# State-space input tables made on GpSimd, and the chunk inputs moved behind the last input projections

## Chip, cores and metric

One core of a Trainium2 chip runs the whole two-layer model in one launch. The metric is the device time of one execution in microseconds. Rows of the profile call the engines PE (TensorE matmul; PEld its weight loads), DVE (VectorE), ACT (ScalarE), POOL (GpSimd) and SP (the queue that issues most DMAs). Each engine runs its own instructions in order, and waits on semaphores for the others.

## The reference

Only layer 0 is touched. There, 1024 latent tokens and 256 context tokens are normalised and modulated (scale and shift from a conditioning vector times a weight matrix `ada_w`), then projected by `w_in`. Columns 0 to 767 of the projection feed a bidirectional state-space recurrence (S5) with 48 groups of 16 channels and 64 complex states, columns 768 to 1023 an FNet branch, columns 1024 to 2047 a SiLU gate.

```python
lam_bar = jnp.exp(lam * step)
b_bar = ((lam_bar - 1.0) / lam)[..., None] * lax.complex(b_re, b_im)
bu = lax.complex(einsum('btgh,gph->btgp', u, b_bar.real), einsum('btgh,gph->btgp', u, b_bar.imag))
_, s = lax.associative_scan(_linear_recurrence, (a, bu), axis=1)
return einsum('btgp,ghp->btgh', s.real, c_re) - einsum('btgp,ghp->btgh', s.imag, c_im)
...
y = concat([glu(gelu(y_s5)), fnet(u_f)]) * silu(z)
xl = xl + gate * (y @ w_out)
```

## The kernel before

The recurrence is done by chunks of 8 tokens. For each group there are **input tables** (powers of `lam_bar` times `b_bar`: 8 tokens of a chunk to the chunk's contribution to the state, tile `bl`) and **output tables** (powers times C, tile `cl`, with strips of the kernel within a chunk, `z`). Twelve input tasks (`bl_task`, 4 groups each) make five element-wise operations of 128x512 on VectorE, then TensorE transposes the result (`pt`), ScalarE copies it (`bltw`) and a DMA stores it to DRAM (`bltd`). Twelve output tasks (`cl_task`) make five operations of 128x576 on VectorE, store `cl` (`cld`), and TensorE multiplies (`pz`); ScalarE and two small VectorE operations (`dg`, `z`) finish the strips. A chunk input (`bl_mm`, twelve) loads a table (`blt`) and the projected tokens (`ub`) again, multiplies them (`vps`), and ScalarE writes the chunk's contribution to `va` (groups 0 to 23) or `vb` (24 to 47).

The order is written out by hand: instructions stand on each engine's queue in the order of the Python calls. In layer 0:

1. First phase: x is loaded, the sums of squares are taken, the coefficients are computed in small VectorE operations between larger ones (`self.inter` with counts), the modulation weights are loaded and multiplied (`ada_mm`), and projections m = 0 and 1 are made as the channel tiles become ready (`first`).
2. Projections m = 2 to 5 of the S5 columns: 8 parts (k) of six 128x512 matmuls each, 48 in all, since weights and data are split into high and low halves (`whi`, `wlo`; `hh`, `hl`) for accuracy; the weight of the next projection is split on ScalarE and VectorE (`w_split`). Each is followed by the context's product (`uc`). Between the parts `fill()` runs a task's TensorE part and starts the next task, first the twelve input tasks, then the twelve output tasks, with two in flight:

```python
def fill():
    flush()
    if len(pend) == 2 or not todo:
        if pend:
            pend.pop(0)()
    if todo:
        f, b, hf = todo.pop(0)
        ...
```

3. The first FNet projection `fx(0)` with the first six chunk inputs between its parts, then the other six alone.
4. Tree and scan on VectorE: `tree` merges the context's chunks, `step` advances one chunk of one half of the groups; 121 pairs of steps stand behind the second FNet projection `fx(1)` and the eight gate projections (m = 8 to 15) on TensorE. Splits for these run on GpSimd.
5. Output stage (`yps`), which needs the last scan step; then the FNet, the GLU and layer 1, which the change leaves alone.

Weights come through a ring of four buffers (`raw`); six of the first loads have places of their own (`self.place`, tiles `hh2` to `hh7` before these are needed).

Of the kernel before, what the change touches and what calls it, by code (L numbers as in the profile page):

```python
# [30 lines left out]
# ------------------------------------------------------------------ constants that depend on shapes  # L31
# [151 lines left out]
class Builder:  # L183
# [64 lines left out]
    # ---------------------------------------------------------------- streamed weights  # L248
# [51 lines left out]
    def w_issue(self, upto=-1):  # L300
        """Loads: those that the ring has room for or that have a place of their own, and all up to the given one."""
# [23 lines left out]
    def w_split(self, name, eng=None, hi=None, lo=None, parts=1, c0=0, c1=None):  # L325
        """The stationary tile's exact high and low parts (columns c0 .. c1, of those that were left)."""
# [44 lines left out]
    # ---------------------------------------------------------------- accurate exp on DVE  # L371
# [20 lines left out]
    def cmul(self, orr, oi, ar, ai, br, bi, t1, t2):  # L392
        self.mul(t1, ar, br)
        self.mul(t2, ai, bi)
        self.mul(orr, ar, bi)
        self.mul(oi, ai, br)
        self.add(oi, oi, orr)
        self.sub(orr, t1, t2)

    # ---------------------------------------------------------------- S5 tables  # L400
    def s5_prelim(self, tp, s5s, raw):
# [21 lines left out]
        self.ts(sh, sh, -2.0, 1.0, ALU.mult, ALU.add)  # L423
        pw = tp.tile([P, 4, 9, NG], F32, name="pw")
        nc.vector.memset(pw[:, 0, 0], 1.0)
        nc.vector.memset(pw[:, 3, 0], 0.0)
# [4 lines left out]
        w2 = tp.tile([P, 4, NG], F32, name="w2")  # L431
        for n in (1, 2, 4):
# [7 lines left out]
            self.cmul(o[0], o[1], a[0], a[1], b(pw[:, 0, n]), b(pw[:, 3, n]), u1, u2)  # L440
        self.sub(pw[:, 1], pw[:, 3], pw[:, 0])
        self.add(pw[:, 2], pw[:, 3], pw[:, 0])
        # (lam_bar - 1) / lam
        den, xr, cr, ci = step, r, th, er
        self.mul(den, lre, lre)
        self.mul(t1, lim, lim)
        self.add(den, den, t1)
        nc.vector.reciprocal(den, den)
        self.ts(xr, lr, -1.0, None, ALU.add)
        self.mul(cr, xr, lre)  # L450
        self.mul(t1, li, lim)
        self.add(cr, cr, t1)
        self.mul(cr, cr, den)
        self.mul(ci, li, lre)
        self.mul(t1, xr, lim)
        self.sub(ci, ci, t1)
        self.mul(ci, ci, den)
        self.bb = self.kp.tile([P, 2, NG + 1, 16], F32, name="bb")
        self.bbs = self.gp.tile([P, NG, 16], F32, name="bbs")

        def inputs():
            """B times (lam_bar - 1) / lam, and the sum of its parts: the operations, one by one."""
            nc.vector.memset(self.bb[:, :, NG], 0.0)
            bbr, bbi = self.bb[:, 0, 0:NG], self.bb[:, 1, 0:NG]
            x = [tp.tile([P, T], F32, tag="sq", name="x1", bufs=2)[:, 0:NG * 16].rearrange("p (g h) -> p g h", g=NG)
                 for _ in range(2)]
            br, bi = (x.unsqueeze(2).to_broadcast([P, NG, 16]) for x in (cr, ci))
            for out, a, b, op in ((bbr, raw[:, 0], br, ALU.mult), (x[0], raw[:, 1], bi, ALU.mult),
# [8 lines left out]
        self.pwc = self.kp.tile([P, 3, 9, NG], F32, name="pwc")  # L477
        self.acf = self.pwp.tile([P, 2, 2, NG], F32, name="acf")

        def tables(i):  # L480
            for ri in range(3):
                if i == 0:
                    self.act(self.pwb[0:64, ri], pw[0:64, ri, 0:8][:, ::-1])
                    self.act(self.pwb[64:128, ri], pw[64:128, ri, 0:8])
# [6 lines left out]
        return tables, inputs  # L491

    def bl_task(self, b, hf):
        """Chunk input matrices of 4 groups, transposed, to DRAM: (vector part, tensor part)."""
# [4 lines left out]
        def dve():  # L499
            p = self.gt.tile([P, 4, 16, 8], F32, tag="blp", name="blp", bufs=1)  # L500
            B = [x[:, g4].unsqueeze(3).to_broadcast([P, 4, 16, 8]) for x in (self.bbs, self.bb[:, 0], self.bb[:, 1])]
            W = [self.pwb[:, i, :, g4].rearrange("p s g -> p g s").unsqueeze(2).to_broadcast([P, 4, 16, 8])
                 for i in range(3)]
# [228 lines left out]
    def layer0(self, es):  # L732
# [187 lines left out]
        for x in rest:  # L920
            if not isinstance(x, int):
                x()
# [700 lines left out]
```

## Time and profile before

| | us |
|---|---|
| median of 3 runs (lowest, highest) | 947.33 (946.02, 950.22) |
| span of the profiled execution | 943.4 |
| TensorE busy | 888.9 (94%) |
| VectorE busy | 589.4 (62%) |
| ScalarE busy | 315.9 (33%) |
| GpSimd busy | 93.8 (10%) |

The profile is of one execution; the median of the runs lies 3.9 us above its span, which holds the instructions from the first to the last. Busy shares are averages over stages with different limits, so they are read stage by stage. A row of the busy times by stage gives the stretch, its length, then us and number of instructions for PE, PEld, DVE, ACT and POOL, the granted TensorE clock, the DMA share and GB/s. A row of the timeline gives start, duration of the group, engine, line of the kernel, operation, output<-inputs, shapes, count and, in brackets, the idle time before it with what ended it.

### The profile page before, as it was taken

The page shows a single profiled execution, that of the slowest core. Times are in us where ns is not written, and L with a number is a line of the kernel's source. Part 1 is how long each engine was busy: PE and PEld are TensorE (multiplying, and loading weights), DVE is VectorE, ACT ScalarE, POOL GpSimd, SP SyncE. Part 2 cuts the span into 40 slices and gives each one's busy share as a digit, 9 for nine tenths or more (in the row PEclk, how much of TensorE's full clock was granted, in tenths as well). Part 3 has the DMA queues.
Part 4 walks back from the last instruction along what each step waited for, and adds up shares of the span by engine and source line. Part 5 has one row for each costly group of instructions (what it writes and reads, how often), then busy time and mean ns, then how long its engine had stood idle before and what let it go on. Part 6 is the DMA issues. An engine that isn't in the chain of part 4 may idle for free.

```text
span 943.4 us, 13977 instructions
## 1 busy us (share of the span) xinstructions
PE 888.9 (94%) x5432; PEld 725.6 (77%) x5432; DVE 589.4 (62%) x1563; ACT 315.9 (33%) x535; POOL 93.8 (10%) x91
## 2 busy tenths in 40 slices
PE   8998788898999958899999999999999999999996
PEld 3666566677777748887888999877888888888995
DVE  7788998767999996656367476254321343335355
ACT  5546331346212109744342244212111222233110
POOL 0002221131221303200043000100000000000000
PEclk9999999999999988999999999999999999999998
DMA  9734557994455466931162010201111111111022
GB/s 348 283 134 144 186 171 206 261 358 157 157 201 187 185 210 192 312 138 40 67 263 94 1 42 4 79 23 57 56 38 52 45 45 45 50 64 44 1 90 89
DMA packets 57601, 120.75 MB, mean 128 GB/s; under 512 B 5248, under 2 KB 30000, under 8 KB 57408
## 3 DMA queue, kind: packets, MB, share of 16 engines
q1 hardware_dynamic: 50672, 96.06, 30.2%
q0 software_dynamic: 6864, 23.81, 8.0%
q8 instruction: 42, 0.69, 0.3%
q14 instruction: 23, 0.19, 0.1%
HBM read 95.83 MB, written 24.02 MB: 127 GB/s over the span
## 4 chain that ended last, share of the span: by engine, by line
PE 62%; DVE 24%; DMA 6%; ACT 5%; issue 1%; SPq 1%; DVEq 0%; POOL 0%; ACTq 0%; POOLq 0%
PE acc L360 53%; DVE va L206 11%; DVE bl L206 4%; DVE vb L206 2%; DMA mt<-zd 2%; PE acc L867 2%; ACT vb L231 1%; DMA zd<-z 1%; DVE blp L206 1%; PE yps L1189 1%; ACT sy L231 1%; DVE xt L206 1%; PE pps L1509 1%; DMA ub<-ud 1%; PE rsb L682 1%
## 5 line engine op out<-in xcount | busy, mean ns | idle before, releaser
L360 PE MATMUL acc<-hh,whi 128*128 128x512 f32 (+1 forms) x672 | 211.8, 388 | 1.4 <-ACT whi L231 1.4
L360 PE MATMUL acc<-hl,whi 128*128 128x512 f32 (+1 forms) x672 | 207.1, 382 | 0.0
L360 PE MATMUL acc<-hh,wlo 128*128 128x512 f32 (+1 forms) x672 | 206.7, 381 | 0.1
L360 PEld LDWEIGHTS acc<-hh,whi 128*128 128x128 f32 x672 | 122.7, 188 | 30.4 <-issue 5.8
L360 PEld LDWEIGHTS acc<-hh,wlo 128*128 128x128 f32 x672 | 125.1, 188 | 25.9 <-DVE wlo L206 0.5
L360 PEld LDWEIGHTS acc<-hl,whi 128*128 128x128 f32 x672 | 125.2, 188 | 25.5
L206 DVE TENSOR_TENSOR wlo<-raw,whi 128x1024 fp32r<-128x1024 f32 (+2 forms) x47 | 52.3, 1118 | 50.9 <-ACT whi L231 50.9
L231 ACT ACTIVATE whi<-raw 128x1024 fp32r<-128x1024 f32 (+2 forms) x55 | 53.9, 986 | 50.2 <-issue 29.0
L206 DVE TENSOR_TENSOR va<-va 128x48 f32<-128x48 f32 (+1 forms) x258 | 55.9, 218 | 0.4
L227 DVE SCALAR_TENSOR_TENSOR xl<-acc,adac,xl 128x256 f32<-128x256 f32 (+1 forms) x48 | 27.3, 570 | 41.6 <-PE acc L360 41.3
L360 PE MATMUL acc<-yh,hh 128*128 128x256 f32 (+1 forms) x144 | 46.3, 321 | 0.0
L360 PE MATMUL acc<-hh,wl 128*128 128x256 f32 (+1 forms) x144 | 46.1, 320 | 0.0
L360 PE MATMUL acc<-hh,wh 128*128 128x256 f32 (+1 forms) x144 | 46.0, 320 | 0.0
L360 PE MATMUL acc<-yl,hh 128*128 128x256 f32 (+1 forms) x144 | 45.8, 318 | 0.0
L360 PE MATMUL acc<-yh,hl 128*128 128x256 f32 (+1 forms) x144 | 45.7, 317 | 0.0
L360 PE MATMUL acc<-hl,wh 128*128 128x256 f32 (+1 forms) x144 | 45.6, 317 | 0.0
L1189 PE MATMUL yps<-cl,sy 128*128 128x128 f32 x192 | 32.3, 295 | 12.7 <-ACT sy L231 12.7
L206 DVE TENSOR_TENSOR va<-va,acf 128x96 f32<-128x96 f32 x127 | 38.7, 305 | 0.2
L1189 PEld LDWEIGHTS yps<-cl,sy 128*128 128x128 f32 x192 | 28.0, 210 | 13.2 <-ACT sy L231 13.0
L231 ACT ACTIVATE hh<-xl 128x256 f32<-128x256 f32 (+1 forms) x24 | 11.7, 489 | 70.2 <-DVE xl L227 70.2
L206 DVE TENSOR_TENSOR va<-vb,acf 128x96 f32<-128x96 f32 x127 | 34.2, 269 | 0.2
L1026 PE MATMUL vps<-ub,blt 128*64 128x160 f32 x192 | 28.3, 301 | 3.9 <-DMA ub<-ud 2.5
(264 smaller groups left out, 1630.7 us busy)
## 6 DMA issues: line engine op xcount, KB each, us to landing
raw<-in_ada SPq DMA_DIRECT2D x44, 512.0 KB, 6.2
raw<-in_win SPq DMA_DIRECT2D x38, 512.0 KB, 3.6
raw<-in_wout SPq DMA_DIRECT2D x16, 512.0 KB, 3.5
bltd<-bltw POOLq DMA_DIRECT2D x12, 512.0 KB, 3.2
blt<-bltd SPq DMA_DIRECT2D x12, 512.0 KB, 8.6
cl<-cld POOLq DMA_DIRECT2D x12, 512.0 KB, 6.4
cld<-cl SPq DMA_DIRECT2D x18, 256.0 KB, 4.3
ub<-ud SPq DMA_DIRECT2D x12, 384.0 KB, 7.4
```

The lines of the kernel that those rows point to most:

```text
L206: (eng or self.nc.vector).tensor_tensor(out, a, b, op=op)
L227: self.nc.vector.scalar_tensor_tensor(out, a, s, b, op0=op0, op1=op1)
L231: self.nc.scalar.activation(out, a, func, **kw)
L360: self.nc.tensor.matmul(p, a[:, w], b[:, c0:c1], start=(j == 0 and i == 0), stop=(last and i == 2))
L682: self.nc.tensor.matmul(p2[:, P * i:P * i + P], self.ones, dg[:, i], start=True, stop=True)
L867: nc.tensor.matmul(acc[m][h], a[:, w], b[:, 512 * h:512 * h + 512], start=(k == 0 and i == 0), stop=(k == 7 and i == 2))
L1026: nc.tensor.matmul(ps[0:64, o], blt[:, ri, g, 0:64], ub[:, g, 0:160], start=True, stop=True)
L1189: nc.tensor.matmul(ps[:, o], sy[:, ri, g], cl[:, ri, g], start=False, stop=(ri == 1))
L1509: nc.tensor.matmul(ps, pwt[:, i], pd[:, 4 * h:4 * h + 4].rearrange("p s j -> p (s j)"), start=True, stop=True)
```

## The change

- The coefficient operations of `s5_prelim` behind the sine and the exponential (25, and nine small ones in `inputs`) and the seven of 768 elements that scale B run on GpSimd (`g`), only a reciprocal stays on VectorE. The counted list after `sumsq7` becomes a plain list, in which `inverse`, `inputs` and `tables(0)` have places.
- The twelve input tasks' element-wise part runs on GpSimd. It starts with two tasks; each transposition (`bl_pe`) starts the next task but one. The table of powers is held with the 8 tokens innermost (`pwb`).
- Input and output tasks are two lists, with places by projection and part (`hooks`); an output task starts when the one before it is multiplied.
- Chunk inputs move: the first six behind the parts of `fx(1)`, the others behind parts 0 to 5 of gate projection 8, two loads ahead instead of three. The second half's tree stands behind part 6, and the paired steps begin with projection 9.
- All first-phase modulation weights have places of their own (14 instead of 6); squares go to the `wlo` buffers.
- Stores of tables, projections and FNet inputs are issued by ScalarE instead of GpSimd; output tables' and strips' stores stay on SP throughout.

```diff
-        self.mul(lr, er, sh)
-        self.mul(li, er, sn)
+        self.mul(lr, er, sh, g)
+        self.mul(li, er, sn, g)
...
             for out, a, b, op in ((bbr, raw[:, 0], br, ALU.mult), (x[0], raw[:, 1], bi, ALU.mult),
...
-                self.tt(out, a, b, op)
-                yield
+                self.tt(out, a, b, op, g)
...
-        self.pwb = self.gp.tile([P, 3, 8, NG], F32, name="pwb")
+        self.pwb = self.gp.tile([P, 3, NG, 8], F32, name="pwb")
...
-            self.mul(p, B[0], W[0])
-            self.mul(bl[:, 0], B[2], W[2])
-            self.mul(bl[:, 1], B[1], W[1])
-            self.sub(bl[:, 0], p, bl[:, 0])
-            self.add(bl[:, 1], p, bl[:, 1])
+            self.mul(p, B[0], W[0], eng)
+            self.mul(bl[:, 0], B[2], W[2], eng)
+            self.mul(bl[:, 1], B[1], W[1], eng)
+            self.sub(bl[:, 0], p, bl[:, 0], eng)
+            self.add(bl[:, 1], p, bl[:, 1], eng)
...
-            nc.gpsimd.dma_start(self.bltd[b][:, :, 4 * hf:4 * hf + 4], blt)
+            nc.scalar.dma_start(self.bltd[b][:, :, 4 * hf:4 * hf + 4], blt)
...
-        for i in range(6):
-            self.place[4 + i] = self.hl_tile(f"hh{2 + i}", F32)
+        places = ["hl1", "hh1"] + [f"h{i}{k}" for k in range(2, KD) for i in "hl"]
+        places[4:6] = places[5:3:-1]
+        for i, n in enumerate(places):
+            self.place[4 + i] = self.hl_tile(n, F32)
...
+        def bl_ew():
+            if bls:
+                t = self.bl_task(*bls.pop(0))
+                t[0](nc.gpsimd)
+                blp.append(t[1])
+
+        def bl_pe():
+            blp.pop(0)()
+            bl_ew()
...
+        def cl_next():
             flush()
-            if len(pend) == 2 or not todo:
-                if pend:
-                    pend.pop(0)()
-            if todo:
-                f, b, hf = todo.pop(0)
...
+            if clp:
+                clp.pop(0)()
+            if cls:
+                t = self.cl_task(*cls.pop(0))
                 t[0]()
-                pend.append(t[1])
+                clp.append(t[1])
...
+        hooks = {2: at(k6=[cl_next], k7=[bl_pe]),
+                 3: at(k1=[cl_next], k2=[bl_pe], k4=[cl_next], k6=[cl_next], k7=[bl_pe]),
+                 4: at(k1=[cl_next], k3=[bl_pe], k4=[cl_next], k6=[cl_next]),
+                 5: at(k0=[bl_pe], k1=[cl_next], k3=[cl_next], k5=[bl_pe], k6=[cl_next])}
...
-            nc.gpsimd.dma_start(um[:, :, 32:160], ut.rearrange("p (s j) -> p s j", s=8))
+            nc.scalar.dma_start(um[:, :, 32:160], ut.rearrange("p (s j) -> p s j", s=8))
...
-            if i + 3 < 12:
-                bl_load(i + 3)
+            if i + 2 < 12:
+                bl_load(i + 2)
...
+        fx(0, at(k0=[cl_next], k1=[bl_pe], k2=[cl_next], k3=[bl_pe], k5=[lambda: bl_load(0)], k6=[bl_pe],
+                 k7=[lambda: bl_load(1)]))
+        while clp:
+            cl_next()
...
+        fx(1, at(k0=[bl_next], k1=[bl_pe], k2=[bl_next], k3=[bl_next], k4=[bl_pe], k5=[bl_next], k6=[bl_next],
+                 k7=[bl_next]))
...
-                      hook=lambda k: self.bg(2 if k % 4 else 1))
+                      hook=(lambda k: bl_next() if blk else trees() if k == 6 else None) if m == 8 else lambda k: self.bg(2))
```

On VectorE, where the output tables begin, before the change (`cbs` is a sum of C's parts, `clp` an intermediate product): this stretch stands behind the last input task.

```order
L206 TENSOR_TENSOR bl<-blp,bl 128x512 x2
L206 TENSOR_TENSOR cbs<-cb 128x768
L206 TENSOR_TENSOR clp<-cbs,pwc 128x576
L206 TENSOR_TENSOR cl<-cb,pwc 128x576 x2
L206 TENSOR_TENSOR cl<-clp,cl 128x576
L227 SCALAR_TENSOR_TENSOR cl<-clp,cl 128x576
L206 TENSOR_TENSOR clp<-cbs,pwc 128x576
L206 TENSOR_TENSOR cl<-cb,pwc 128x576 x2
L206 TENSOR_TENSOR cl<-clp,cl 128x576
L227 SCALAR_TENSOR_TENSOR cl<-clp,cl 128x576
L227 SCALAR_TENSOR_TENSOR dg<-cst,vec,pz 128x16
L206 TENSOR_TENSOR z<-z,dg 128x16
```

The same place on VectorE after it, behind the context's modulation:

```order
L206 TENSOR_TENSOR cbs<-cb 128x768
L206 TENSOR_TENSOR wlo<-raw,whi 128x1024
L206 TENSOR_TENSOR clp<-cbs,pwc 128x576
L206 TENSOR_TENSOR cl<-cb,pwc 128x576 x2
L206 TENSOR_TENSOR cl<-clp,cl 128x576
L227 SCALAR_TENSOR_TENSOR cl<-clp,cl 128x576
L206 TENSOR_TENSOR wlo<-raw,whi 128x1024
L227 SCALAR_TENSOR_TENSOR dg<-cst,vec,pz 128x16
L206 TENSOR_TENSOR z<-z,dg 128x16
L206 TENSOR_TENSOR clp<-cbs,pwc 128x576
L206 TENSOR_TENSOR cl<-cb,pwc 128x576 x2
```

The input tasks are gone from this queue, and the first `dg`, which needs TensorE's product of the first output task, now stands ahead of the second output task instead of behind it.

On GpSimd, behind the first phase, after the change (`bbs` is the last of the seven operations that scale B); before, only DMA issues stood there.

```order
L206 TENSOR_TENSOR bb<-bb,x_539 128x768
L206 TENSOR_TENSOR bbs<-bb 128x768
L206 TENSOR_TENSOR blp<-bbs,pwb 128x512
L206 TENSOR_TENSOR bl<-bb,pwb 128x512 x2
L206 TENSOR_TENSOR bl<-blp,bl 128x512 x2
```

The last three of these rows are one input task; twelve follow one another, with one split ahead of the last.

On SP's queue, where the first chunk inputs are loaded, before the change (`cld` output tables, `zd` strips):

```order
L544 DMA cld_84<-cl 128x4x128 x4
L544 DMA cld_85<-cl 128x4x128 x2
L967 DMA blt<-bltd_78 128x2x512
L969 DMA ub<-ud_96 128x4x192
L967 DMA blt<-bltd_78 128x2x512
L969 DMA ub<-ud_96 128x4x192
L544 DMA cld_85<-cl 128x4x128 x2
```

And after it:

```order
L545 DMA cld_89<-cl 128x4x128 x2
L950 DMA zd_94<-z 128x2x240
L545 DMA cld_89<-cl 128x4x128 x2
L967 DMA blt<-bltd_78 128x2x512
L969 DMA ub<-ud_96 128x4x192
L967 DMA blt<-bltd_78 128x2x512
L969 DMA ub<-ud_96 128x4x192
L950 DMA zd_95<-z 128x2x240
L310 DMA raw<-in_ada 128x1024
L967 DMA blt<-bltd_79 128x2x512
```

The first loads moved from behind the third output task's stores to behind the twelfth's, and the third chunk input's loads stand behind a weight load.

## Rows read from the trace of the kernel before

**Rows 1.** Busy time of the engines by stage, columns as told above.

```profile
0.00:80.70 80.70, 73.62 (x428) 46.97 (x428) 61.08 (x150) 42.50 (x79) 1.59 (x8) 0.98 0.59 224
80.70:144.50 63.80, 52.77 (x282) 40.59 (x283) 62.18 (x73) 24.60 (x47) 17.90 (x24) 1.00 0.62 191
144.50:209.00 64.50, 57.39 (x742) 44.27 (x742) 47.15 (x106) 23.31 (x56) 11.87 (x15) 1.00 0.95 277
209.00:226.80 17.80, 14.41 (x185) 12.55 (x182) 12.53 (x38) 14.67 (x28) 0.55 (x1) 1.00 0.71 249
...
237.80:353.10 115.30, 106.07 (x644) 78.93 (x642) 115.30 (x727) 20.71 (x43) 21.86 (x14) 0.97 0.55 192
```

**Rows 2.** Chain that ended last: start, us, what; three stretches.

```profile
85.26 0.65 ACT acf L231 x4
...
213.26 12.53 ACT vb L231 x23
...
227.73 0.95 DVE tr L206
...
352.38 0.71 DVE va L206 x5
```

**Rows 3.** Timeline of VectorE and GpSimd around splits; then GpSimd's position table, grouped.

```profile
211.00 1.94 DVE L206 TENSOR_TENSOR va<-va,tr 128x768 f32<-128x768 f32 x2
...
228.60 4.15 DVE L206 TENSOR_TENSOR vb<-vb,tr 128x768 f32<-128x768 f32 x2
...
238.22 0.21 DVE L206 TENSOR_TENSOR va<-va,vb 128x48 f32<-128x48 f32 x1
...
239.05 2.44 DVE L206 TENSOR_TENSOR va<-va,vb 128x48 f32<-128x48 f32 x1
...
227.76 3.19 POOL L206 TENSOR_TENSOR wlo<-raw,whi 128x1024 fp32r<-128x1024 f32 x1 [16.78 <-ACT whi L231]
239.03 2.40 POOL L206 TENSOR_TENSOR wlo<-raw,whi 128x1024 fp32r<-128x1024 f32 x1 [8.08 <-ACT whi L231]
...
L206 POOL TENSOR_TENSOR xl<-xl,cst 128x1024 f32<-128x1024 f32 x7 | 19.5, 2824 | 92.1 <-DMA xl<-in_x 92.1
```

**Rows 4.** VectorE's groups by form: count, busy us, mean ns, idle before.

```profile
L206 DVE TENSOR_TENSOR wlo<-raw,whi 128x1024 fp32r<-128x1024 f32 x37 | 45.2, 1220 | 46.8 <-ACT whi L231 46.8
...
L206 DVE TENSOR_TENSOR bl<-bb,pwb 128x512 f32<-128x512 f32 x24 | 24.9, 1083 | 0.0
L206 DVE TENSOR_TENSOR cl<-cb,pwc 128x576 f32<-128x576 f32 x24 | 17.1, 753 | 10.5 <-DMA cld<-cl 10.1 <-issue 0.4
L206 DVE TENSOR_TENSOR bl<-blp,bl 128x512 f32<-128x512 f32 x24 | 15.5, 689 | 0.0
```

**Rows 5.** Timeline of TensorE, from 82 to 182 us, starts of its pieces.

```profile
82.56 0.63 PE L360 MATMUL acc<-hh,whi 128*128 128x512 f32 x2
...
83.97 0.63 PE L360 MATMUL acc<-hh,whi 128*128 128x512 f32 x2
...
95.05 1.23 PE L515 MATMUL pt<-cst,bl 128*128 128x128 f32 x8 [1.34 <-DVE bl L206]
96.04 0.71 PE L360 MATMUL acc<-hh,whi 128*128 128x512 f32 x2
...
100.28 0.36 PE L360 MATMUL uc<-chh,whi 128*128 128x256 f32 x1
...
103.11 0.28 PE L360 MATMUL uc<-chh,wlo 128*128 128x256 f32 x1
...
179.27 0.35 PE L1026 MATMUL vps<-ub,blt 128*64 128x160 f32 x1
...
181.60 0.81 PE L554 MATMUL pz<-cl,bb 64*32 64x128 f32 x32
```

**Rows 6.** DMA issues: output<-input, queue, count, KB each, median us to landing.

```profile
blt<-bltd SPq DMA_DIRECT2D x12, 512.0 KB, 8.6
...
ub<-ud SPq DMA_DIRECT2D x12, 384.0 KB, 7.4
```

More of the change, by code (lines that the diff above doesn't have):

```diff
@@ L439, in s5_prelim @@
             u1, u2 = (w1[:, 0], w2[:, 0]) if n == 1 else (w1[:, :n], w2[:, :n])
[L440 to L458, printed above, removed]
+            self.cmul(o[0], o[1], a[0], a[1], b(pw[:, 0, n]), b(pw[:, 3, n]), u1, u2, g)
+        self.sub(pw[:, 1], pw[:, 3], pw[:, 0], g)
+        self.add(pw[:, 2], pw[:, 3], pw[:, 0], g)
+        self.bb = self.gp.tile([P, 2, NG + 1, 16], F32, name="bb")
         self.bbs = self.gp.tile([P, NG, 16], F32, name="bbs")
         def inputs():
-            nc.vector.memset(self.bb[:, :, NG], 0.0)
+            self.ts(xr, lr, -1.0, None, ALU.add, eng=g)
+            self.mul(cr, xr, lre, g)
+            self.mul(t1, li, lim, g)
+            self.add(cr, cr, t1, g)
+            self.mul(cr, cr, den, g)
+            self.mul(ci, li, lre, g)
+            self.mul(t1, xr, lim, g)
+            self.sub(ci, ci, t1, g)
+            self.mul(ci, ci, den, g)
+            g.memset(self.bb[:, :, NG], 0.0)
             bbr, bbi = self.bb[:, 0, 0:NG], self.bb[:, 1, 0:NG]
-            x = [tp.tile([P, T], F32, tag="sq", name="x1", bufs=2)[:, 0:NG * 16].rearrange("p (g h) -> p g h", g=NG)
-                 for _ in range(2)]
+            x = [self.slot("x1")[:, 0:NG * 16].rearrange("p (g h) -> p g h", g=NG) for _ in range(2)]
             br, bi = (x.unsqueeze(2).to_broadcast([P, NG, 16]) for x in (cr, ci))
@@ L490, in tables @@
                     self.act(self.acf[:, o[0], o[1]], pw[:, k, 8], scale=sc)
-        return tables, inputs
+        return inverse, tables, inputs
     def bl_task(self, b, hf):
@@ L736, in layer0 @@
         hh, hlo, sq = ([None] * KD for _ in range(3))
[L737 to L738 removed]
+        gx = ExitStack()
+        self.gp = gx.enter_context(tc.tile_pool(name="gp", bufs=1, side="right"))
         pwx = ExitStack()
         self.pwp = pwx.enter_context(tc.tile_pool(name="pwp", bufs=1))
[L741 to L744 removed]
+        kx = ExitStack()
+        chp = kx.enter_context(tc.tile_pool(name="chp", bufs=1))
+        chh = [chp.tile([P, TC], F32R, name=f"chh{k}") for k in range(KD)]
+        chl = [chp.tile([P, TC], F32R, name=f"chl{k}") for k in range(KD)]
         sx = ExitStack()
@@ L917, in layer0 @@
-        self.cnt = 1
-        tables, inputs = self.s5_prelim(xp, s5s, rawb)
-        rest, self.inter = self.inter, []
-        for x in rest:
-            if not isinstance(x, int):
-                x()
-        tables(0)
-        inputs = inputs()
-        for _ in range(4):
-            next(inputs)
-        ax = ExitStack()
+        self.inter += [2, sumsq7]
+        self.cnt = 1
+        inverse, tables, inputs = self.s5_prelim(xp, s5s, rawb)
+        for f in [
+                rs_r, mm(0), row(0), rs_a(0), rs_d(0), mm(1), row(1), rs_a(1), rs_d(1), w(0, 0, 128),
+                fin(0), rs_p(0), fin(1), rs_p(1), mm(2), mod_0, row(2), first(0, (0,)), mod_t(1), w(0, 128),
+                w(1, 0, 256), mod_h(1), mm(3), row(3), first(0, (1,)), fin(2), mod_l(1), inverse, first(1), inputs,
+                mod_t(2), w(1, 256), fin(3), mod_h(2), mod_t(3), mod_l(2), mod_h(3), mm(4), row(4), first(2),
+                mod_l(3), fin(4), mm(5), row(5), first(3), fin(5), lambda: tables(0),
+                mod_t(4), mod_t(5), mod_h(4, 5), mod_l(4), mod_l(5), mm(6), row(6), first(4), mm(7), row(7), fin(6),
+                ctx_q, first(5), fin(7), mod_t(6), mod_t(7), mod_h(6, 7), mod_l(6), mod_l(7), ctx_s, ctx_row,
+                first(6), ctx_r, ctx_b, first(7), ctx_mod(0, 1), ctx_mod(2, 3), ctx_mod(4, 5), ctx_mod(6, 7)]:
+            f()
@@ L931, in hr @@
         def hr(k):
             return hh[k], hlo[k]
-        todo = []
-        for b in range(6):
-            todo += [(self.bl_task, b, 0), (self.bl_task, b, 1)]
-        for b in range(6):
-            todo += [(self.cl_task, b, 0), (self.cl_task, b, 1)]
-        pend = []
         self.zq = []
         self.sq = nc.sync
+        bls, cls = [divmod(i, 2) for i in range(12)], [divmod(i, 2) for i in range(12)]
+        blp, clp = [], []
+        def bl_ew():
[3 more added lines that the diff above has]
+                blp.append(t[1])
@@ L1104, in layer0, with trees @@
             square(l)
-        while blk:
-            bl_mm(blk.pop(0))
-            if len(blk) == 0:
-                self.w_split(names[8], nc.gpsimd)
-            if len(blk) < 5:
-                tree(0, 4 - len(blk))
+        for l in range(5):
+            tree(0, l)
         for i in range(NC_, NC_ + SKEW):
             step((0, i))()
-        for l in range(5):
-            tree(1, l)
         n = NSTEP - 1
+        def trees():
+            for l in range(5):
+                tree(1, l)
         self.bgq = [step((0, i + SKEW), (1, i)) for i in range(NC_, n - SKEW)]
         rest = [step((1, i)) for i in range(n - SKEW, n)]
-        store = fx(1, lambda k: self.bg(2 if k % 4 else 1))
-        zt = [self.slot(f"zt{k}") for k in range(KD)]
+        zt = []
         gates = [(0, ch) for ch in range(8, 12)] + [(1, ch) for ch in range(12)]
@@ L1124, in layer0 @@
             k = m - 8
+            zt.append(self.slot(f"zt{k}"))
             hl = self.w_take(names[m])
```

121 lines of the change are left out of this document (52 added, 69 removed).

## Prediction

> **What bounds the kernel now.** I read the busy time by stage first [rows 1]. From 80.7 to 144.5 us, where the twelve input tables are made, VectorE is busy 62.2 of 63.8 us and TensorE only 52.8. From 144.5 to 209.0 (output tables, first chunk inputs) TensorE has 57.4 of 64.5, and 14.4 of 17.8 up to 226.8. From 237.8 to 353.1 VectorE is busy without a gap: that is the scan. Then the chain of waits [rows 2]. The chunk inputs' evacuations run until 226.8, the tree over the second half's context chunks follows at once, and the scan ends at 353.09; the output stage waits for it. So everything later hangs on one event, **the end of the last chunk input at 226.8 us**. From there 126.3 us of VectorE work follow, in both kernels. I forecast where that event goes.
>
> **TensorE's own sum up to that event.** One of eight parts of a projection takes 83.97 - 82.56 = 1.41 us, one transposition of a table 96.04 - 95.05 = 0.99, the context's product 2.95 (100.28 to 103.11 and the last one's length), a chunk input 181.60 - 179.27 = 2.33, an output table's products 0.81 [rows 5]. Before: five projections, four context products, twelve of each other kind: 56.4 + 11.8 + 11.9 + 9.7 + 28.0 = 117.8, with 2.2 for the last evacuations (four of the 23 in 12.53 us [rows 2]) 120.0. From 80.7 that is 200.7, so TensorE lost 26.1 us to waits. The change moves the second FNet projection and six of the eight parts of the first gate projection ahead of the event: 14 x 1.41 = 19.7. Without any wait it would come at 220.4, only 6.4 earlier. The gain is small even if all of the waits go; the question is what waits the new order has.
>
> **Input tables on GpSimd.** VectorE loses 60 operations of 512 elements, 36 of 1.08 and 24 of 0.69 us [rows 4], 55 us. What does GpSimd need for one? Its only two-input operation here takes 2.40 us for 1024 elements undisturbed, 2.82 beside VectorE [rows 3]. So 1.20 for 512, with the wait between a task's dependent operations 1.25; bounds 1.1 and, if the mixed broadcast patterns cost double, 2.5. The nearest row has such a pattern too (the position table added to xl), so I take 1.25: 6.25 per task, 75 us in all.
>
> The main term is that the two engines do not run beside each other. A scan operation of 0.21 us takes 2.44 when it meets GpSimd's split of 2.40, which began 0.02 before; two tree operations that take 1.94 elsewhere take 4.15 beside a split, and this split takes 3.19, since it waited for VectorE first [rows 3]. Each blocks the other for whole instructions, and they alternate. All table operations on VectorE have two inputs in SBUF, as these had, and so have the splits. The Trainium skill says this as a rule (SBUF — State Buffer, "Who interferes with whom"): a VectorE instruction with two SBUF inputs contends with a GpSimd instruction that reads SBUF, and the later one is blocked until the first ends. By that rule the trace agrees, and the sum is the one that follows; without the rule it would be the second rival.
>
> So from the third projection to the end of the first FNet projection one access is shared by: nine input tasks, 9 x 6.25 = 56.3; twelve output tasks of five operations, 60 x 0.753 = 45.2 [rows 4]; five splits of 1.22, 6.1; one sum of 768 wide, about 0.9. Together 108.5 us. TensorE's sum there is 40 x 1.41 + 11.8 + 9 x 0.99 + 9.7 = 86.8. The tasks can't start much earlier: they follow the copies into the scan tables, which ended at 85.9 before [rows 2]. Nor is all of it in reserve: an output task is now emitted behind the small operations of the one before, so only one is in flight. Where two lie two parts (2.82 us) apart, VectorE needs 5 x 0.753 and half a us for the small ones, 4.3; three such places cost 4.5 and one of 3.8 some 0.5. I take 108 for the stage; lower bound 92 (86.8 and those 5), upper 120 (the idle places of the shared access on top).
>
> GPSIMD Engine Reference ("2.1 Instruction dispatch") gives a floor of 2.5 cycles per element with two inputs: an estimate from it is 1.07 us for 512 elements, the stage 100 instead of 108, and the end 8 us earlier than the sum here; the row of 2.40 stands above that floor.
>
> **First phase.** The small operations of the coefficients leave VectorE, but seven of 768 elements (2.40 x 0.75 = 1.8 each, 12.6 us) now block it while it modulates the channel tiles. Modulation weights with own places come without waiting for a free buffer; TensorE has only 7.1 us free there [rows 1] for that to take away. The squares now share the splits' two places; TensorE's sums of squares free them in turn, so that costs nothing. I take the third projection's start at 82 instead of 80.7; bounds 78 and 88.
>
> **Chunk inputs.** Loads of the first two now stand on SP's queue behind the last output task's stores (before: behind the second's). The chunk input waits for a load that is issued when that task is done, about 1 us ahead of the projection's end, and lands 7.4 to 8.6 us after issue [rows 6]; one part covers 1.4: 7 us of wait (bounds 3 and 11). Then 14 x 1.41 + 3 x 0.99 + 12 x 2.33 = 50.7. Further loads on SP's queue stand behind two weight loads whose buffer a GpSimd split must free: 3 us at the gate projection (0 to 6). The last evacuations: 2.2.
>
> **Queues.** 32 stores (tables, projections) go from GpSimd's queue to ScalarE's; it is busy 24.6 of 63.8 and 23.3 of 64.5 us [rows 1], which hides them. If not, each place where an evacuation stands behind one costs a fraction of a us, and 10 us at most if all were exposed at a third of a us. Of the work behind the event, two of the eight GpSimd splits that blocked VectorE for 2.2 each [rows 3] now come ahead of it (the projections' parts that they make are the same): -4.4.
>
> **The sum.** 82 + 108 + 7 + 50.7 + 3 + 2.2 = 252.9, against 226.8: +26.1; less 4.4 is +21.7. The profiled span is 943.4, so 965.1; the median of the runs shown is 3.9 above that span, which I keep: 969.
>
> **Rivals.** *Faster: the waits go and no new ones come.* For: VectorE is the only bound in the first of these stages, and 55 us leave it. Then the event is at 220.4, and with the 4.4 the time is 936.5. Against: the blocked operations of [rows 3]. It decides below a stage of S us: 82 + S + 7 + 50.7 + 5.2 = 231.2 gives S = 86.3, under TensorE's own 86.8; so the loads' wait would have to go as well. *Same or a little slower: GpSimd runs beside VectorE at no cost, and the rest of my waits stand.* The stage is 92: 236.9 at the event, +5.7 in all, 953; with the first phase unchanged 952, with half the load wait as well 948. For: the transpositions lie 10 us apart on the average (nine in 87), more than a task needs alone, and the blocking is seen only with GpSimd operations of 1024 elements. *Much slower: GpSimd at 2.5 us per operation.* Twelve tasks need 150 us, with the 52 us of VectorE's share some 200 from 82, then 6 parts with a chunk input (22.4) and 5: over 1020. Against: the row of 2.40.
>
> **How the numbers follow.** Shared access 0.60 (likeliest, 969; its own range 958 to 985), waits gone 0.15 (936), no cost beside VectorE 0.17 (953, from 947 to 958), doubled GpSimd 0.08. A measurement of this kernel tells some 0.5% from no change, that is 942.6 to 952.1. Faster: 0.15. Same: the lower part of the third case, 0.10. Slower: 0.60 + 0.08 + 0.07 = 0.75. The range from 940 to 985 leaves out most of the second case and of the last, with the likeliest one's upper end.
>
> **What would show it.** Right: between 82 and 190 us VectorE's output-table operations of 0.75 us are seen at 1.5 to 2, GpSimd's at 1.25 to 2; TensorE waits for cl on VectorE several times by 1 to 5 us; the last chunk input is evacuated at about 250; the scan still takes about 110 us; TensorE stands idle 25 to 35 us at its end. Wrong: cl operations at 0.75 beside busy GpSimd, or an event before 232. The sum fails by a term if the first phase moves by more than 5 us, or if the first chunk input does not wait for its load.

## The result and the profile after

The changed kernel takes 992.40 us (median of 4 runs, 986.42 to 994.25), the kernel before 947.82 beside it: 1.047 of the time before (95% interval 1.043 to 1.051). Slower, as forecast, but by 45 us instead of 22, and outside the range of 940 to 985. The profiled span is 988.9, 45.5 more than before.

Busy time of the changed kernel in five stretches, with the columns of [rows 1]: to the third projection, to the first chunk input, to the last chunk input's evacuation, the trees and the scan, the rest.

```profile
0.00:90.64 90.64, 78.08 (x429) 50.84 (x430) 58.24 (x110) 45.29 (x79) 34.88 (x51) 0.92 0.53 204
90.64:213.10 122.46, 99.91 (x800) 77.36 (x799) 78.16 (x90) 33.44 (x75) 78.21 (x56) 0.90 0.68 176
213.10:273.40 60.30, 53.71 (x491) 43.81 (x492) 20.77 (x63) 33.67 (x58) 10.00 (x7) 0.97 0.70 234
273.40:395.20 121.80, 97.42 (x607) 71.96 (x605) 121.49 (x746) 19.54 (x41) 19.11 (x12) 0.92 0.50 173
395.20:988.90 593.70, 575.14 (x3110) 495.68 (x3110) 280.38 (x452) 188.29 (x283) 36.85 (x29) 0.98 0.24 77
```

The chain of waits has the same hinge as in [rows 2]: last evacuation, tree, scan, output stage.

```profile
272.86 0.51 ACT vb L231
...
273.40 1.05 DVE tr L206 x2
...
394.49 0.71 DVE va L206 x5
```

So the event came at 273.4 instead of 226.8 (+46.6). From there to the scan's end it is 121.8 us instead of 126.3 (-4.5, forecast -4.4), and from the scan's end to the end 593.7 instead of 590.3 (+3.4, not forecast; it was 589 to 592 in the runs below whose output stage waits for the scan, so part of it is scatter). The error is in the event: forecast 252.9. By the terms of the sum: third projection at 90.6 instead of 82 (+8.6); table stage 119.9 instead of 108, without the load's wait (+11.9); that wait 2.5 instead of 7 (-4.5); from the first chunk input to the last evacuation 60.3 instead of 50.7 + 3 + 2.2 (+4.4). Together 20.4 of the 20.5.

The timeline of the changed kernel shows three of these places: the first phase at 53 us, one output task at 165 us, and the loads at 246 us.

```profile
53.68 5.47 ACT L231 ACTIVATE pwb<-pw 64x384 f32<-64x384 f32 x6
59.17 2.19 ACT L231 ACTIVATE hh<-xt,adac 128x1024 fp32r<-128x1024 f32 x2
...
60.37 1.22 PE L874 MATMUL acc<-hh,whi 128*128 128x512 f32 x2 [6.03 <-ACT hh L231]
61.39 1.05 PE L874 MATMUL acc<-hh,wlo 128*128 128x512 f32 x2
...
66.97 0.72 PE L874 MATMUL acc<-hh,whi 128*128 128x512 f32 x2
...
166.82 3.12 POOL L206 TENSOR_TENSOR bl<-blp,bl 128x512 f32<-128x512 f32 x2
...
168.07 0.75 DVE L206 TENSOR_TENSOR clp<-cbs,pwc 128x576 f32<-128x576 f32 x1
...
168.73 3.35 DVE L206 TENSOR_TENSOR cl<-cb,pwc 128x576 f32<-128x576 f32 x2
170.01 1.46 POOL L206 TENSOR_TENSOR blp<-bbs,pwb 128x512 f32<-128x512 f32 x1
172.01 0.74 DVE L206 TENSOR_TENSOR cl<-clp,cl 128x576 f32<-128x576 f32 x1
...
172.90 1.72 PE L555 MATMUL pz<-cl,bb 64*32 64x128 f32 x32 [4.18 <-DVE cl L206]
...
174.55 1.22 PE L360 MATMUL acc<-hh,whi 128*128 128x512 f32 x2
...
175.23 0.23 DVE L227 SCALAR_TENSOR_TENSOR dg<-cst,vec,pz 128x16 f32<-128x16 f32 x1 [1.80 <-ACT z L231]
...
245.95 2.40 POOL L206 TENSOR_TENSOR wlo<-raw,whi 128x1024 fp32r<-128x1024 f32 x1 [23.31 <-ACT whi L231]
...
248.38 0.34 SPq L310 DMA_DIRECT2D raw<-in_ada  x1
...
249.44 0.55 SPq L969 DMA_DIRECT2D ub<-ud  x1
...
256.66 0.50 PE L1028 MATMUL vps<-ub,blt 128*64 128x160 f32 x1 [5.68 <-DMA ub<-ud]
```

First place: ScalarE copies the powers into `pwb` ahead of the fifth channel tile's high part, and TensorE stands idle for 6.03 us. Behind that its pairs of products take 1.05 instead of 0.63: the granted clock was 0.50 from 60.4 to 64.0 us, the lower one of two levels (half clock). Second: two output-table operations take 3.35 us between GpSimd's operations; two undisturbed take 1.42 in the same run. TensorE waits 4.18 for them and again goes on at half clock (1.22). From the start of the product (172.90) to the small operation `dg` that VectorE has to do before the next task it is 2.33 us. Third: a weight load stands on SP's queue until a GpSimd split is done at 248.35 (245.95 + 2.40), and the chunk input's loads behind it.

Its groups by form (count, busy us, mean ns, idle before) and TensorE's waits in the two middle stretches:

```profile
L206 POOL TENSOR_TENSOR bl<-blp,bl 128x512 f32<-128x512 f32 x24 | 36.5, 1542 | 0.0
L206 POOL TENSOR_TENSOR bl<-bb,pwb 128x512 f32<-128x512 f32 x24 | 32.7, 1384 | 40.2 <-PE pt L516 40.2
L206 DVE TENSOR_TENSOR cl<-cb,pwc 128x576 f32<-128x576 f32 x24 | 27.7, 1193 | 0.0
```

```profile
PE pz L555 <- DVE cl L206: 15.0, 6, 4.2
PE vps L1028 <- DMA ub<-ud: 8.2, 2, 5.7
PE pz L555 <- DVE cl L227: 4.9, 6, 1.2
```

The operation of 0.753 in [rows 4] has a mean of 1.193 here. TensorE waits 19.9 us for output tables (15.0 + 4.9).

### The profile page after: what moved, and what is told of

It is laid out like the page before. It is cut to its first block, busy times and chain, and to the rows that moved or that the text cites. A ratio compares the mean times of both kernels' runs of the same rounds, so it can differ in the third digit from the quotient of the medians.

```text
span 988.9 us, 13963 instructions
## 1 busy us (share of the span) xinstructions
PE 904.3 (91%) x5432; PEld 739.7 (75%) x5432; DVE 559.0 (57%) x1459; ACT 320.2 (32%) x535; POOL 179.1 (18%) x154
## 4 chain that ended last, share of the span: by engine, by line
PE 61%; DVE 13%; DMA 3%; ACT 1%; issue 0%; DVEq 0%; SPq 0%; ACTq 0%
PE acc L360 52%; DVE va L206 9%; PE vps L1028 2%; DVE vb L206 2%; PE yps L1191 2%; DMA mt<-zd 1%; PE yps L1189 1%; DMA zd<-z 1%; DMA ub<-ud 1%; PE pps L1511 1%; DVE tr L206 1%; PE ytr L1202 1%; PE rsb L683 0%; PE pzf L1273 0%; PE pa L1299 0%; PE ssum L657 0%
## 5 line engine op out<-in xcount | busy, mean ns | idle before, releaser
L360 PE MATMUL acc<-hh,whi 128*128 128x512 f32 (+1 forms) x672 | 215.2, 394 | 0.0
L206 DVE TENSOR_TENSOR wlo<-raw,whi 128x1024 fp32r<-128x1024 f32 (+2 forms) x47 | 54.0, 1155 | 60.9 <-ACT whi L231 60.9
L206 DVE TENSOR_TENSOR va<-va 128x48 f32<-128x48 f32 (+1 forms) x258 | 60.5, 235 | 0.4
L1191 PE MATMUL yps<-cl,sy 128*128 128x128 f32 x192 | 33.7, 304 | 27.9 <-ACT sy L231 26.6
L227 DVE SCALAR_TENSOR_TENSOR xl<-acc,adac,xl 128x256 f32<-128x256 f32 (+1 forms) x48 | 27.3, 570 | 41.6 <-PE acc L360 41.3
L206 POOL TENSOR_TENSOR bl<-bb,pwb 128x512 f32<-128x512 f32 x24 | 32.7, 1384 | 40.2 <-PE pt L516 40.2
L206 POOL TENSOR_TENSOR wlo<-raw,whi 128x1024 fp32r<-128x1024 f32 x8 | 19.3, 2416 | 110.3 <-ACT whi L231 110.3
L206 POOL TENSOR_TENSOR bl<-blp,bl 128x512 f32<-128x512 f32 x24 | 36.5, 1542 | 0.0
```

What stands on the lines that cost most here:

```text
L206: (eng or self.nc.vector).tensor_tensor(out, a, b, op=op)
L227: self.nc.vector.scalar_tensor_tensor(out, a, s, b, op0=op0, op1=op1)
L360: self.nc.tensor.matmul(p, a[:, w], b[:, c0:c1], start=(j == 0 and i == 0), stop=(last and i == 2))
L1191: nc.tensor.matmul(ps[:, o], sy[:, ri, g], cl[:, ri, g], start=False, stop=(ri == 1))
```

## The experiments

The first seven look at the stretch from the third projection to the first chunk input; a table stands behind six of them. Ratios are to the kernel before.

**Copies of the powers late.** Short diff against the changed kernel:

```diff
-                mod_l(3), fin(4), mm(5), row(5), first(3), fin(5), lambda: tables(0),
+                mod_l(3), fin(4), mm(5), row(5), first(3), fin(5),
...
+                mod_l(6), mod_l(7), lambda: tables(0), ctx_s, ctx_row,
```

> The changed kernel (992.4 us), with the six copies of the input tables' powers on ScalarE (5.47 us together, at 53.7) moved from ahead of the fifth channel tile's high part to behind the last tile's. Theory: TensorE's wait of 6.03 us at 60.4 and the half clock behind it (some 2.5 us) come from these copies alone. Then the third projection starts at 82 to 83 instead of 90.6, and the time is 983 to 986. Rival: the first phase is longer because GpSimd's coefficient operations block VectorE (splits and modulations of 2.2 instead of 1.28); then a wait of some 4 us stays at this place and the time is above 988.

985.90 us, 1.041 (1.038 to 1.045). The wait of 6.03 us falls to 0.54, so the copies caused it; but the third projection starts at 86.8, only 3.8 earlier: TensorE now waits 1.94 for the context's sums (a wait of 1.67 right behind that stood in the changed kernel too). And the first chunk input does not move (213.16): waits for output tables are 22.1 instead of 19.9 us, and the clock 0.88. The 2.6 us by which the profiled span is shorter came from behind the scan, which the edit doesn't touch. So the place was right and the gain was given back. That the time lies in the first theory's 983 to 986 is luck: the projection start that it rests on, 82 to 83, was missed.

**Output tasks one ahead.**

```diff
-            if cls:
+            for _ in range(2 if len(cls) == 12 else min(1, len(cls))):
                 t = self.cl_task(*cls.pop(0))
```

> The changed kernel, with two output tasks started at the first place, so that each is made one place ahead of its product. Theory of the prediction (VectorE and GpSimd share one access): the work to be shared stays 108 us, so the stretch from the third projection to the first chunk input falls from 120 only to 108 to 112 us, and the time to 980 to 985. Rival (the chain from a product over ScalarE's strip and two small VectorE operations to the next five operations is what TensorE waits for): the waits for cl fall from 20 us to under 5, the half clock behind them goes with them, the stretch is 90 to 95 us, and the time 962 to 970.

981.65 us, 1.037 (1.034 to 1.040), the time that the shared access gave. TensorE's waits for output tables fall from 19.9 to 9.2 us (7.3 for `cl` at L206, 1.9 at L227). The stretch is 113.1 us, and without the load's wait 105.2, on either side of the forecast 108 to 112. So one task in flight instead of two costs 14.7 us beside GpSimd, not 5.

**No input-table operations.**

```diff
-            self.mul(p, B[0], W[0], eng)
...
-            self.add(bl[:, 1], p, bl[:, 1], eng)
+            eng.memset(bl.rearrange("p r g h s -> p (r g h s)"), 0.0)
```

> The changed kernel, with the five GpSimd operations of each input task replaced by one that writes zeros (the tables, and so the chunk inputs, are left out). Theory of the prediction (shared access): the output tasks' operations take 0.75 us throughout, TensorE's waits for cl fall from 20 us to under 3, and the stretch from the third projection to the first chunk input from 120 to 88 to 92 us; time 960 to 966. Rival (the chain from product to next task): VectorE's operations take 0.75 but waits of 5 to 10 us stay, with half clock behind them; stretch 98 to 105 us, time 970 to 980.

968.45 us, 1.024 (1.020 to 1.027). VectorE's operations take 0.75 throughout, and 21.1 us of the stretch go. But waits of 7.5 us for output tables (6.4 + 1.1) stay with nobody to share with. The rows show one cycle of an output task there, from one product to the next:

```profile
PE pz L550 <- DVE cl L206: 6.4, 6, 2.2
PE vps L1023 <- DMA ub<-ud: 2.4, 1, 2.4
PE pz L550 <- DVE cl L227: 1.1, 6, 0.3
```

```profile
115.05 0.41 PE L550 MATMUL pz<-cl,bb 64*32 64x128 f32 x4 [0.70 <-DVE cl L206]
...
116.94 0.23 DVE L227 SCALAR_TENSOR_TENSOR dg<-cst,vec,pz 128x16 f32<-128x16 f32 x1 [1.37 <-ACT z L231]
...
117.30 0.75 DVE L206 TENSOR_TENSOR clp<-cbs,pwc 128x576 f32<-128x576 f32 x1
...
120.11 0.41 PE L550 MATMUL pz<-cl,bb 64*32 64x128 f32 x4 [0.78 <-DVE cl L206]
```

The rival holds in the waits and in the stretch (98.8 us); its time, 970 to 980, is missed by 1.5 us. The length of 0.75, which both had forecast, shows that GpSimd's operations had made VectorE's longer; the first theory's stretch of 88 to 92 us and its time do not come.

**Input tables back on VectorE.** `t[0](nc.gpsimd)` becomes `t[0](nc.vector)`.

> The changed kernel, with the five operations of each input task back on VectorE at the same places of the program. Theory of the prediction (shared access, so where the operations run matters little): VectorE does 9 x 4.6 + 45 + 7 = 94 us in the stretch behind which TensorE waits in places; stretch 105 to 118 us, time 975 to 990, some 10 us under the changed kernel. Rival (GpSimd takes work off VectorE as far as it goes): VectorE's own queue gets longer, the waits for cl grow by the 4.6 us of each input task, stretch over 130 us and time over 1000.

980.40 us, 1.036 (1.033 to 1.038): 10 us less of the stretch than on GpSimd, within the shared-access forecast.

**The changed kernel mended,** with GpSimd and with VectorE. Besides the first two edits:

```diff
-        fx(0, at(k0=[cl_next], k1=[bl_pe], k2=[cl_next], k3=[bl_pe], k5=[lambda: bl_load(0)], k6=[bl_pe],
-                 k7=[lambda: bl_load(1)]))
+        fx(0, at(k0=[cl_next], k1=[bl_pe], k2=[cl_next, lambda: bl_load(0)], k3=[bl_pe], k4=[lambda: bl_load(1)], k6=[bl_pe]))
...
+        def gate8(k):
+            if blk:
+                bl_next()
+            if k == 3:
+                self.w_split(names[9], nc.gpsimd)
...
```

> The changed kernel with the copies of the powers late (as in the first run), the output tasks one ahead (as in the second), the first two chunk-input loads three places earlier, and the split for gate projection 9 behind the last chunk-input loads. Input tables on GpSimd as in the change. Theory (what is left is the shared access, 108 us of work from the third projection): first chunk input at 195 to 200 us, no wait of 5 us for a load, last evacuation at 249 to 253, time 966 to 969. Rival (waits and half clock were the loss, the shared access is not): first chunk input at 180 to 185, time 950 to 954.

> The run before this one, with the input tables' operations on VectorE (0.685 us each). Theory (shared access): VectorE's sum in the stretch is 9 x 3.4 + 45 + 7 = 83, below TensorE's 87, so the first chunk input comes at 180 to 185 us, and the time is 950 to 955: 15 us less than with GpSimd. Rival (GpSimd runs beside VectorE once output tasks are one ahead): equal to the run with GpSimd within 4 us.

With GpSimd 968.10 us, 1.021 (1.019 to 1.024); with VectorE 948.36, 1.001 (1.000 to 1.003). This pair differs in the engine of 60 operations alone: 20 us, so the second forecast's rival (equal within 4 us) is out. In the stretch it is 105.0 against 88.2 without the load's wait, 16.8 us; the sum had 108 against TensorE's own 86.8, or 92 with the 5 us for one task in flight, which this pair no longer has. The wait of 5.7 us at the gate projection is gone in both. The first load's wait is 7.7 and 3.3, so the forecast "no wait of 5 us for a load" fails with GpSimd, and the first chunk input (201.0) and the last evacuation (255.8) come later than forecast although the time was met.

Windows of the stretch in these runs, each kernel's row as in the first block: late copies,

```profile
86.80:213.16 126.36, 102.01 (x800) 78.81 (x799) 78.02 (x90) 33.32 (x75) 78.42 (x56) 0.88 0.66 171
```

one ahead,

```profile
92.05:205.15 113.10, 93.85 (x800) 73.25 (x799) 88.26 (x90) 33.42 (x75) 87.47 (x57) 0.93 0.75 199
```

no input-table operations,

```profile
90.53:191.76 101.23, 91.37 (x800) 71.64 (x799) 53.97 (x97) 33.10 (x75) 12.17 (x12) 0.98 0.83 212
```

on VectorE,

```profile
90.56:202.20 111.64, 96.97 (x801) 75.47 (x799) 85.27 (x146) 32.97 (x75) 1.37 (x1) 0.92 0.73 192
```

mended with GpSimd,

```profile
88.33:201.01 112.68, 93.47 (x801) 72.68 (x799) 88.71 (x90) 33.31 (x75) 87.11 (x57) 0.93 0.76 201
```

and mended with VectorE:

```profile
87.04:178.54 91.50, 87.92 (x800) 69.64 (x799) 85.77 (x146) 32.88 (x75) 2.59 (x1) 1.00 0.89 236
```

| | stretch | first load's wait | stretch without it | TensorE busy | clock |
|---|---|---|---|---|---|
| changed kernel | 122.5 | 2.5 | 119.9 | 99.9 | 0.90 |
| copies late | 126.4 | 2.2 | 124.1 | 102.0 | 0.88 |
| one ahead | 113.1 | 7.9 | 105.2 | 93.9 | 0.93 |
| no input-table operations | 101.2 | 2.4 | 98.8 | 91.4 | 0.98 |
| on VectorE | 111.6 | 2.1 | 109.6 | 97.0 | 0.92 |
| mended, GpSimd | 112.7 | 7.7 | 105.0 | 93.5 | 0.93 |
| mended, VectorE | 91.5 | 3.3 | 88.2 | 87.9 | 1.00 |

TensorE does the same 800 instructions in each. At full clock they take 87.9 us (last row; the sum had 86.8). In the changed kernel they take 12.0 more, at a mean granted clock of 0.90; the next run shows that it is the waits that bring it down. A wait costs its length and what it does to the clock.

**Small products in the waits.**

```diff
             if clp:
+                fill = self.ps("acc", "fill")
+                for _ in range(16):
+                    nc.tensor.matmul(fill[:, 0:P], self.ones, self.ones, start=True, stop=True)
                 clp.pop(0)()
```

> The changed kernel, with 16 small products without use ahead of each output task's product, so that TensorE does not stand idle while it waits for the task. Theory (half clock behind the waits costs the stretch 13 us of its 120): the granted clock of the stretch rises from 0.90 to over 0.96, its length falls by 3 to 8 us, time 984 to 989. Rival (the stretch follows the shared access and TensorE's speed hardly matters there): the clock rises, but the length changes by less than 2 us or grows by what the small products take, time 990 to 998.

1005.32 us, 1.060 (1.059 to 1.061).

```profile
90.06:226.80 136.74, 130.68 (x1184) 114.35 (x1183) 74.72 (x100) 33.35 (x75) 79.91 (x57) 0.99 0.62 165
```

The time lies above both forecasts. The clock rose to 0.99 and the waits for output tables fell to 1.4 us, so it is the idle time that brings the clock down. But the products were chosen too long: 130.7 less the 87.9 of TensorE's own work is 43 us, more than the waits and the half clock that they replaced. What the clock alone is worth in time stays open.

**The old order with only the input tables on GpSimd** (`self.mul(p, B[0], W[0], nc.gpsimd)` and so on; 8 tokens innermost; stores on ScalarE's queue).

> The kernel before with only the input tables' operations on GpSimd (8 tokens innermost, stores of tables and projections on ScalarE's queue), everything else in its old order. Here VectorE has only weight splits and the first output tables to do beside them. Theory (GpSimd alone is slower than VectorE on these operations: 1.07 undisturbed, some 1.25 with splits): twelve tasks take 64 to 75 us from 87 on, the output tables begin 8 to 16 us later, time 955 to 963. Rival (two engines share the work): TensorE's own 53 us bound the stage, time 937 to 942.

969.32 us, 1.023 (1.021 to 1.026): slower even than the first theory had it. GpSimd's timeline shows one task, and TensorE's waits what came of it:

```profile
101.35 1.07 POOL L206 TENSOR_TENSOR blp<-bbs,pwb 128x512 f32<-128x512 f32 x1
102.38 2.10 POOL L206 TENSOR_TENSOR bl<-bb,pwb 128x512 f32<-128x512 f32 x2
104.44 2.48 POOL L206 TENSOR_TENSOR bl<-blp,bl 128x512 f32<-128x512 f32 x2
107.00 1.07 POOL L206 TENSOR_TENSOR blp<-bbs,pwb 128x512 f32<-128x512 f32 x1
```

```profile
PE pt L514 <- POOL bl L206: 21.7, 21, 2.4
```

Undisturbed, a task is 5.65 us (107.00 - 101.35): 1.07 for a product and 1.25 for a sum, where VectorE takes 0.685 and 3.4 a task in that layout. Twelve tasks took from 89.0 to 164.0, the 75 us of the forecast's upper end. The time was missed by the waits, which that forecast counted only as a later end of the tables. The next run has the same layout and these operations on VectorE: 936.1 against 969.3, so the move to GpSimd, with the stores on ScalarE's queue, costs 33 us in the old order.

**The old order with 8 tokens innermost, all on VectorE.**

```diff
-        self.pwb = self.gp.tile([P, 3, 8, NG], F32, name="pwb")
+        self.pwb = self.gp.tile([P, 3, NG, 8], F32, name="pwb")
...
-            W = [self.pwb[:, i, :, g4].rearrange("p s g -> p g s").unsqueeze(2).to_broadcast([P, 4, 16, 8])
-                 for i in range(3)]
+            W = [self.pwb[:, i, g4].unsqueeze(2).to_broadcast([P, 4, 16, 8]) for i in range(3)]
```

> The kernel before (947 us) with one thing of the change: the table of powers held with the 8 tokens innermost, so that the input tables' operations read both inputs in rows. In the run with these operations back on VectorE they took 0.685 us instead of 1.083, so VectorE's 62.2 us in the stage from 80.7 to 144.5 fall by 12 x 3 x 0.40 = 14, and the copies into that table take 2 us more. Theory (that stage is bound by VectorE, TensorE's own work there is 53): the last chunk input comes 8 to 10 us earlier, and the time is 937 to 940. Rival (what VectorE saves is waited for at the output tables): 944 to 947.

936.09 us, 0.988 (0.986 to 0.990), slightly under the first theory's range: the one part of the change that was tried alone and gains. The mended kernel with VectorE (948.36) has this layout too, with the rest of the change, and is 12 us slower; which part of the rest costs that was not taken apart. The groups of this run by form and TensorE's one longer wait up to 92 us:

```profile
L206 DVE TENSOR_TENSOR bl<-bb,pwb 128x512 f32<-128x512 f32 x24 | 15.4, 685 | 0.0
```

```profile
PE acc L360 <- ACT whi L231: 3.9, 1, 3.9
```

The operation of 1.083 in [rows 4] is done in 0.685. The copies into that table take 0.9 each on ScalarE instead of 0.52, and the third projection waits 3.9 us behind them.

**The same, with the copies earlier** (`ctx_r, lambda: self.tables0(), first(5)`, in ScalarE's idle time).

> The old order with the 8 tokens innermost (936.1 us), with the six copies into that table ahead of the context's modulation, where ScalarE stood idle from 64.1 to 68.9 us before, instead of behind it. There TensorE waited 3.9 us for the weight split behind these copies (5.67 us together). Theory: the wait falls to some 1 us, the copies delay the context's modulation by up to 1 us, and the time is 933 to 934. Rival (the output tables' and loads' waits behind it take up the gain, as in the run with the copies moved alone): 935 to 937.

931.17 us, 0.983 (0.981 to 0.986). The wait of 3.9 is gone; better than forecast by 2 us. **This version beats both kernels.**

**Splits of the gate projections on VectorE,** on top of that: `self.w_split(names[m + 1])` without `nc.gpsimd`. In the second run the hooks hand out `self.bg(2 if k % 2 else 1)`.

> The run before this one, with the seven weight splits of gate projections 9 to 15 on VectorE instead of GpSimd. Theory (a GpSimd split stops VectorE's scan for its whole length: five scan steps of 0.70 us take 2.90 where one falls): each split takes 1.22 from the scan instead of 2.2, so the scan is 7 x 1.0 = 7 us shorter; time 926 to 928. Rival (on VectorE's queue the split waits for ScalarE's high part, or TensorE then waits for it because VectorE lags): no gain, 932 to 938.

> The run with the splits on VectorE (943.5 us), with fewer scan steps handed out per part of a projection (12 instead of 14 in eight parts), so that VectorE does not fall behind TensorE and the splits, and with them the weight buffers, come in time. Theory (VectorE's lag made the loads late; TensorE waited 15 us for weights): the waits fall under 4 us, the scan ends at 330 to 334, time 925 to 930. Rival (VectorE has too little slack for any pace): waits of 8 us and more stay, time 934 to 943.

The first: 943.50 us, 0.996 (0.994 to 0.998): 12 us lost, by the rival's mechanism but more than its 932 to 938. TensorE's wait in that stage, and SP's queue: of the two weight loads in its row the second is issued almost 20 us after the first, since its buffer is held until VectorE's late split is done at 235.6:

```profile
PE adaps L576 <- DMA raw<-in_ada: 15.2, 7, 5.0
```

```profile
216.00 19.92 SPq L310 DMA_DIRECT2D raw<-in_ada  x2
```

With the slower pace 931.61 us, 0.984 (0.982 to 0.986): no measurable difference to the splits on GpSimd. The paired scan steps do end earlier, at 330.0 instead of 337.6 us, as the theory had it. But TensorE still waits 6.0 us for weights in that stage, where it waited for none with the splits on GpSimd, and is not done with the projections before 336.6; ScalarE's `sy`, which the output stage needs, follows at 337.0 (337.6 with the splits on GpSimd):

```profile
330.04 0.64 DVE L1176 COPY sy<-va 64x512 f32<-64x512 f32 x1
...
336.55 0.49 PE L1186 MATMUL yps<-mt,ul 128*128 128x128 f32 x2
...
336.97 4.30 ACT L231 ACTIVATE sy<-va 64x512 f32<-64x512 f32 x4
```

Neither theory's time holds: what the scan gains by the move is lost to late loads, and moving the splits is worth nothing here.

## Why the prediction was wrong, step by step

- **Shared access (right as a mechanism; its size partly by luck).** With one task in flight it was to cost 108 - 92 = 16 us; the run without the operations has 21.1. With tasks ahead it was to cost 108 - 86.8 = 21; the pair of mended runs has 16.8. GpSimd's 1.25 per operation undisturbed was 1.07 to 1.25. The rival "GpSimd beside VectorE at no cost" is out. The Trainium skill's rule (SBUF — State Buffer, "Who interferes with whom") holds on these rows: an operation of 0.75 takes some 1.6 where GpSimd reads SBUF ahead of it (3.35 for two at 168.73). But the sum counted nine input tasks, and GpSimd makes eleven in the changed kernel's stretch (the row below), two ahead of their transpositions. With eleven tasks of 5.65, the undisturbed length in the old order, the sum's terms make 114.4 us, an estimate from these rows; so that 105 us came out near 108 is no proof of the sum's size.

```profile
L206 POOL TENSOR_TENSOR blp<-bbs,pwb 128x512 f32<-128x512 f32 x11 | 13.8, 1258 | 37.6 <-ACT acf L231 36.8
```

- **One task in flight (failed: the sum took it at nothing).** The 108 us are the work on the shared access alone, as if it never stood idle. The 5 us for one task in flight stood only in the lower bound of 92, and the idle places only in the upper bound of 120, where the stage came out (119.9). With one task in flight VectorE has no table operation to make between a task's last one and the next `dg`. The price of 5 us was too low too: "VectorE needs 5 x 0.753 and half a us for the small ones, 4.3" against two parts of 2.82 left out what lies ahead of the small operations, the product and ScalarE's strip. In the run with nothing to share, a cycle is 5.06 us (115.05 to 120.11), 1.89 of it from the product to `dg`, against two parts and a product, 3.6; in the changed kernel the way to `dg` took 2.33 at 172.90. Measured: 14.7 us, 6.0 of it TensorE's busy time at the lower clock (99.9 - 93.9).
- **Half clock (left out).** The sum took each wait by its length. TensorE's work in the stretch grew by 12.0 us, and its products behind the wait at 60 us and behind the load at 256 us ran at half clock too. The clock before was 1.00 in these stages [rows 1], so they could not show it; the output stage before, behind 11.4 us of idle time, could have (0.92 from 353.1 to 427.0).
- **First phase (failed).** "I take the third projection's start at 82": the step priced VectorE, GpSimd and the weights' places, and not ScalarE's queue, on which `tables(0)` had come to stand ahead of the fifth tile. It starts at 90.6. TensorE is busy 78.1 us in this phase instead of 73.6, at a clock of 0.92 instead of 0.98, and idle 12.6 instead of 7.1. The copies are 3.8 us of that, by the first run; the rest (VectorE behind GpSimd may be part of it) was not taken apart. The figure is rough: the phase ended between 90.1 and 92.1 in the runs that leave it alone. In the changed kernel these 3.8 us were given back by the first chunk input; with tasks one ahead they were not (88.3 against 92.0 at the third projection, 201.0 against 205.2 at the chunk input).
- **Loads (half right).** The wait moved: 2.5 instead of 7 at the first chunk input, since its two loads were issued at 204.08 and 206.02, 6.5 and 4.5 us ahead of TensorE's arrival (213.10 - 2.54 = 210.56) and not 1. With tasks one ahead it was 7.9. At the gate projection it was 5.7 instead of 3, by the mechanism named (a weight load whose buffer a split must free). The rest of that last term's error was not taken apart; TensorE is busy 53.7 us there, where the sum had 50.7.
- **Queues (right).** The stores on ScalarE's queue were to be hidden. In the mended run with VectorE they stand there too, and TensorE is idle for 3.6 us of the stretch (91.5 - 87.9), 3.3 of them the load's wait.
- **The event's far side (right).** -4.4 forecast, -4.5 measured: two of the eight blocking splits have gone ahead of the event. TensorE idle for 26.6 us at the scan's end, forecast 25 to 35.
- **What was not seen.** The layout of `pwb` stood in the diff, and the row of 1.083 beside 0.689 for equal sizes [rows 4] showed that reading across that table cost something. I priced the operations only for GpSimd. That row was the gain: 14 us of VectorE's busiest stage.

## What to carry to other kernels

An engine that looks free is not, if its operands come through the access of the engine that is to be relieved: price its operations as added to the other engine's, and ask first whether the operation can be made cheaper where it is. Where a task is emitted only behind the product of the one before, add up the whole cycle over all engines, the small copies too, and compare it with what the waiting engine has to do meanwhile. Whatever moves in the program order moves on every queue: go through ScalarE's and SP's rows as well as those of the engines that the change names.

## Hardware seen on the way

- VectorE, 512 elements, two SBUF inputs: 1.083 us where one input is read with a step of 192 bytes, 0.685 where 8 elements lie together. ScalarE's copy that writes with a step took 0.90 instead of 0.52 for 384. The Trainium skill (SBUF — State Buffer, a note in "Door 1: The DMA port swizzle") says that each access to another line of 16 bytes pays a penalty; these rows agree, and give its size here.
- GpSimd, 512 elements, undisturbed: 1.07 us for a product and 1.25 for a sum or difference of the same shape. I have no run that tells why they differ; the products read two broadcast inputs, the sums two plain ones.
